# Two of w_ada's column blocks (j = 8 and 9) summed by VectorE instead of by column-grouped matmuls on TensorE

## The chip, the cores and the metric

One core of a Trainium2 chip runs the whole kernel. The metric is device microseconds of one execution, the median over several runs. Every time below is in microseconds (us) unless it is marked ns. The engines are called PE (TensorE matmul), PEld (its weight loads), DVE (VectorE), ACT (ScalarE), POOL (GpSimd) and SP (SyncE, which here only issues DMAs).

## The reference, cut to what matters

The kernel is one decoder layer on 512 tokens of 1024 channels. Its conditioning is one row of 6144 numbers:

```python
mod = jnp.einsum('bd,de->be', jax.nn.silu(c), w_ada[l]) + b_ada[l]
sh_m, sc_m, gt_m, sh_f, sc_f, gt_f = jnp.split(mod[:, None, :], 6, axis=-1)
...
u = layer_norm(x) * (1.0 + sc_f) + sh_f
```

With c of shape (1, 1024), this is a product of a vector with a 1024 x 6144 matrix in float32. Around it stand an input projection, two causal mixers (softmax attention with a forget bias, and an RG-LRU), an output projection and a mixture of 16 experts.

## The kernel before, in words

**Blocks of w_ada.** The 6144 columns are cut into twelve blocks j = 0 to 11 of 512 columns. Block j holds half of one of the six vectors: 0 and 1 sh_m, 2 and 3 sc_m, 4 and 5 gt_m, 6 and 7 sh_f, 8 and 9 sc_f, 10 and 11 gt_f. Each block comes in four quarters kh = 0 to 3 of 256 rows, 512 KB a DMA, which lie in SBUF as tile `wa` of 128 x 2 x 512 float32 (`ada_quarter`, L250 to L253). silu(c) lies in the tile `cb`, 128 x 8 x 32, each value repeated over 32 columns.

**Two ways to sum a block.** The string `ADA_BY` (L277) has one letter for each quarter of blocks 4 to 11, four to a block. `ada_acc(j, kh, w)` (L282 to L313) reads it. With "E" the quarters are gathered in pairs, and after kh = 1 and after kh = 3 PE runs four matmuls (L290; the trace has two instructions for each, so groups of eight), each with a stationary operand of 128 x 32 that writes one of four groups of 32 partitions of a PSUM tile; after kh = 3 ACT copies the PSUM tile to a tile `part` (L293). With "D" POOL zeroes `part` at the first quarter (L299), and each quarter costs two DVE instructions, `part = w[:, k, :] * cb[:, k] + part`, 128 x 512 (L305). Both leave a tile of 128 partitions that a later matmul sums over the partitions and turns into columns: `ada_T` (L315 to L323), whose column of weights for the sum is `s4` (one of each 32 partitions) for "E" and `ones1` for "D".

**When blocks are loaded and summed.** Blocks 0 to 3 are summed on PE at the start. From the first projection of the v columns on, each call of `proj()` takes up two quarters (`ada_next`, L482 to L491; `proj`, L493 to L510): blocks 6 and 7 go with the four v projections, block 8 with the projections of q and k of the first head pair (called q0 and k0 here), two quarters each. In `proj()` the quarters of a "D" block are summed by `ada_acc` ahead of that projection's matmuls in program order, and those of an "E" block behind them. Blocks 9, 10 and 11 stand in the hand-written list `TAIL` (L39 to L44): `AL` loads a quarter, `AC` sums one. Its beginning is

```python
AL, AL, pj(1, 0), AC, AC, AL, AL, pj(1, 1), AC, AC, T[0], S[1], N[1], AU[6], pj(2, 0), LW["L"], AL, GW("L", 0, V), GW("L", 1, V), FW["L"][0], pj(2, 1), AL, T[1], PV[0], S[2], AU[7], N[2], AC, AC,
```

Here `pj(i, 0)` and `pj(i, 1)` are the projections of q and k of head pair i; `S[n]` the logits of attention unit n (PE L851, L853, L856), their maximum (DVE L858) and exponential (ACT L861); `N[n]` the normalising (DVE L868, L871); `T[n]` the transposes of the probabilities (PE L883) and their split into a high and a low part (ACT L97, DVE L98); `PV[n]` the products with v; `LW`, `GW` and `FW` load, scale and split rows of w_out (DVE L743, ACT L748, DVE L749); `AU[j]` uses a finished block.

**What a projection waits for.** A projection's weight tile `wi` is loaded three projections ahead (`win_load`, L353 to L359): SP issues the DMA (L355), ACT makes the high part (L357), DVE the low part `wlo` (L358), and PE multiplies high and low parts in three products (L101 to L103). At its end ACT and DVE bring the result from PSUM into a pair of tiles (`qk_evac`: L665 and L666 for q, L668 and L669 for k).

**What sets the order.** The raw tiles `wa`, `wi` and `wo` share five buffers, so each load on SP waits until an earlier raw tile's last reader is done. SP and PE run in program order throughout. ACT, DVE and POOL are ordered by the framework's planner up to the point where `TAIL` begins (block 8 falls there), and in the order of the list from there on (block 9 falls there).

Of the kernel before, what the change touches and what calls it, by code (L numbers as in the profile page):

```python
# [47 lines left out]
def block_kernel(ctx, tc, x, c, w_ada, b_ada, w_in, b_f, conv_w, conv_b, w_rg, b_rg, w_ig, b_ig,  # L48
# [44 lines left out]
    def ps(shape=(128, 512), dt=F32):  # L93
        return pp.tile(list(shape), dt, tag="ps", name=nm("ps"))
# [155 lines left out]
    def ada_quarter(j, kh, src=None, eng=None):  # L250
        w = src[kh] if isinstance(src, list) else raw([128, 2, 512], "wa", src)
        (eng or SP).dma_start(w, w_ada[0, kh * 256:(kh + 1) * 256, j * 512:(j + 1) * 512].rearrange("(k p) n -> p k n", p=128))
        return w  # L253
# [20 lines left out]
    shfT, scfT = sfT[:, 0:8], sfT[:, 8:16]  # L274


    ADA_BY = "EEEEEEEEDDDDDDDDEEEEEEEEEEEEEEEE"  # L277
    parts = {}

    part_q, part_p = {}, {}  # L280
# [1 line left out]
    def ada_acc(j, kh, w):  # L282
        if ADA_BY[(j - 4) * 4] == "E":
            part_q.setdefault(j, []).append(w)
            if kh % 2 == 0:
                return
            if kh == 1:
                part_p[j] = ps()
            for k in range(4):
                T.matmul(part_p[j][32 * k:32 * k + 32, :], cb[:, 2 * kh - 2 + k, :], part_q[j][kh - 1 + k // 2][:, k % 2, :], start=kh == 1, stop=kh == 3)  # L290
            if kh == 3:
                parts[j] = t2k([128, 512], F32, "part")
                A.copy(parts[j], part_p[j])  # L293
                if j in (4, 5, 10, 11):
                    A.dma_start(parts[j][1:2, :], b_ada[0:1, j * 512:(j + 1) * 512])
            return
        if j not in parts:
            parts[j] = t2k([128, 512], F32, "part")
            G.memset(parts[j], 0.0)  # L299
            if j in (4, 5, 10, 11):  # L300
                A.dma_start(parts[j][0:1, :], b_ada[0:1, j * 512:(j + 1) * 512])
        how, ck = ADA_BY[(j - 4) * 4 + kh], cb[:, 2 * kh:2 * kh + 2, 0:1]
        if how == "D":
            for k in range(2):
                V.scalar_tensor_tensor(parts[j], w[:, k, :], ck[:, k, :], parts[j], op0=OP.mult, op1=OP.add)  # L305
            return
        if how == "A":
            for k in range(2):
                A.mul(w[:, k, :], w[:, k, :], ck[:, k, :])
        else:  # L310
            G.tensor_mul(w, w, ck.to_broadcast([128, 2, 512]))
        for k in range(2):
            G.tensor_add(parts[j], parts[j], w[:, k, :])  # L313

    def ada_T(j, part, sel_=None):  # L315
        p = ps()
        for b in range(4):
            T.matmul(p[:, b:b + 1], part[:, b * 128:(b + 1) * 128], s4 if sel_ is None else sel_, start=True, stop=True)  # L318
        o, b0, dst, shift = (j % 2) * 4, *{0: (8, shT, True), 1: (16, sc1T, False), 3: (64, shfT, True), 4: (72, scfT, False)}[j // 2]
        if shift:  # L320
            V.tensor_add(dst[:, o:o + 4], p[:, 0:4], vt[:, b0 + o:b0 + o + 4])
        else:
            V.scalar_tensor_tensor(dst[:, o:o + 4], p[:, 0:4], 1.0, vt[:, b0 + o:b0 + o + 4], op0=OP.add, op1=OP.add)  # L323
# [158 lines left out]
    def ada_next(n):  # L482
        late = []
        for j, kh in ada_rest[:n]:
            a = j, kh, ada_quarter(j, kh)
            if ADA_BY[(j - 4) * 4] == "E":
                late.append(a)
# [22 lines left out]
    def ada_row2(j, part):  # L510
        p = ps()
        T.matmul(p, (s5 if ADA_BY[(j - 4) * 4] == "E" else ones1).to_broadcast([128, 128]), part, start=True, stop=True)
        o = slice((j % 2) * 512, (j % 2) * 512 + 512)
        if j < 6:
            V.tensor_scalar(gtm[:, o], p, 1.0, None, op0=OP.add)
        else:
            A.activation(gtf[:, o], p, AF.Identity, bias=1.0)
# [548 lines left out]
    def ada_use(j):  # L1066
        return lambda: ada_T(j, parts[j], None if ADA_BY[(j - 4) * 4] == "E" else ones1) if j < 10 else ada_row2(j, parts[j])

# [796 lines left out]
```

## Time and profile before

| what | value |
|---|---|
| median of 3 runs | 655.67 us (652.84 to 656.31) |
| the profiled execution's own time | 654.58 us |
| its span from first to last instruction | 652.8 us |
| PE busy | 600.1 us, 92% of the span |
| DVE busy | 453.3 us, 69% |
| ACT busy | 322.3 us, 49% |
| DMA | 165.65 MB, mean 254 GB/s |

How to read it: an engine's busy time is the union of its instructions' spans. The chain of waits is followed back from the last instruction, at each step to what released it. In a timeline, a line is: start, duration, engine, source line, operation, tiles, count, and in brackets the idle time of the engine before it and what ended that idle time. "granted clock" is the share of TensorE's full clock in a stretch.

### The profile page before, as it was taken

The page shows a single profiled execution, that of the slowest core. Times are in us where ns is not written, and L with a number is a line of the kernel's source. Part 1 is how long each engine was busy: PE and PEld are TensorE (multiplying, and loading weights), DVE is VectorE, ACT ScalarE, POOL GpSimd, SP SyncE. Part 2 cuts the span into 40 slices and gives each one's busy share as a digit, 9 for nine tenths or more (in the row PEclk, how much of TensorE's full clock was granted, in tenths as well). Part 3 has the DMA queues.
Part 4 walks back from the last instruction along what each step waited for, and adds up shares of the span by engine and source line. Part 5 has one row for each costly group of instructions (what it writes and reads, how often), then busy time and mean ns, then how long its engine had stood idle before and what let it go on. Part 6 is the DMA issues. An engine that isn't in the chain of part 4 may idle for free.

```text
span 652.8 us, 10217 instructions
## 1 busy us (share of the span) xinstructions
PE 600.1 (92%) x3537; PEld 440.2 (67%) x3537; DVE 453.3 (69%) x740; ACT 322.3 (49%) x512; POOL 180.0 (28%) x186
## 2 busy tenths in 40 slices
PE   4798999999999999989899999999999899999990
PEld 0455877777886888879677776676667577766550
DVE  6757869845744677787798576938686785895264
ACT  0344797344436364644577454445545464753150
POOL 8800002100000000142155353435354343743000
PEclk9899999999999999997899999999999899999996
DMA  9996136996347305375799979799989999999523
GB/s 311 340 266 201 36 117 196 283 276 199 115 166 285 113 4 191 110 278 197 234 332 380 389 233 349 271 328 350 359 285 346 367 377 363 370 385 368 151 104 124
DMA packets 90862, 165.65 MB, mean 254 GB/s; under 512 B 9351, under 2 KB 29943, under 8 KB 90808
## 3 DMA queue, kind: packets, MB, share of 16 engines
q1 hardware_dynamic: 84080, 150.06, 66.2%
q0 software_dynamic: 5024, 10.70, 6.3%
q10 hardware_dynamic: 1704, 4.21, 1.8%
q8 instruction: 29, 0.48, 0.3%
q14 instruction: 25, 0.20, 0.1%
HBM read 156.58 MB, written 12.39 MB: 259 GB/s over the span
## 4 chain that ended last, share of the span: by engine, by line
PE 62%; DMA 18%; DVE 10%; ACT 5%; issue 3%; ACTq 0%; POOL 0%; SPq 0%; POOLq 0%; DVEq 0%
PE ps L101 12%; PE ps L102 12%; PE ps L103 12%; PE ps L1418 7%; DMA er<-in_w_e_up_dram 6%; DMA er<-in_w_e_down_dram 4%; DMA er<-in_w_e_gate_dram 4%; DVE wlo L812 3%; PE ps L1434 2%; DMA wa<-in_w_ada_dram 2%; PE ps L290 2%; DMA wi<-in_w_in_dram 1%; PE ps L318 1%; ACT pr L861 1%; PE ps L883 1%
## 5 line engine op out<-in xcount | busy, mean ns | idle before, releaser
L812 DVE TENSOR_TENSOR wlo<-er,whi 128x1024 fp32r<-128x1024 f32 x91 | 143.9, 1600 | 28.8 <-ACT whi L811 27.1
L811 ACT CAST whi<-er 128x1024 fp32r<-128x1024 f32 x120 | 125.3, 1049 | 73.7 <-PE ps L103 67.0
L812 POOL TENSOR_TENSOR wlo<-er,whi 128x1024 fp32r<-128x1024 f32 x29 | 74.8, 2579 | 76.8 <-ACT whi L811 76.6
L101 PE MATMUL ps<-uh,whi 128*128 128x512 f32 x160 | 64.4, 403 | 0.0
L102 PE MATMUL ps<-wlo,xth 128*128 128x512 f32 x144 | 58.1, 403 | 5.1 <-POOL wlo L812 4.1
L103 PE MATMUL ps<-uh,wlo 128*128 128x512 f32 x160 | 62.6, 392 | 0.0
L102 PE MATMUL ps<-ul,whi 128*128 128x512 f32 x160 | 62.5, 390 | 0.0
L101 PE MATMUL ps<-whi,xth 128*128 128x512 f32 x144 | 58.9, 409 | 0.0
L1418 PE MATMUL ps<-er,xT 128*64 128x256 f32 x512 | 58.8, 382 | 0.0
L103 PE MATMUL ps<-whi,xtl 128*128 128x512 f32 x144 | 57.6, 400 | 1.2 <-DVE xtl L98 1.2
L1418 PEld LDWEIGHTS ps<-er,xT 128*64 128x64 f32 x512 | 35.4, 137 | 19.4 <-issue 1.9
L326 POOL TENSOR_TENSOR rA<-rA,nhalf 128x1 f32<-128x1 f32 x4 | 2.2, 549 | 157.0 <-DVE rA L917 157.0
L101 PEld LDWEIGHTS ps<-uh,whi 128*128 128x128 f32 x160 | 30.1, 188 | 11.9 <-issue 3.9
L358 DVE TENSOR_TENSOR wlo<-wi,whi 128x1024 fp32r<-128x1024 f32 x20 | 25.5, 1275 | 16.9 <-ACT whi L357 16.9
L102 PEld LDWEIGHTS ps<-wlo,xth 128*128 128x128 f32 x144 | 27.4, 190 | 12.7 <-POOL wlo L812 5.8
L357 ACT CAST whi<-wi 128x1024 fp32r<-128x1024 f32 x20 | 21.0, 1048 | 29.0 <-DMA wi<-in_w_in_dram 20.6
L102 PE MATMUL ps<-wlo,hth 128*128 128x512 f32 x80 | 32.6, 407 | 2.6 <-DVE wlo L812 2.6
L103 PEld LDWEIGHTS ps<-uh,wlo 128*128 128x128 f32 x160 | 30.0, 188 | 6.9 <-DVE wlo L358 0.5
L102 PEld LDWEIGHTS ps<-ul,whi 128*128 128x128 f32 x160 | 30.1, 188 | 6.5 <-issue 0.5
L101 PE MATMUL ps<-whi,hth 128*128 128x512 f32 x80 | 33.0, 412 | 0.0
L103 PEld LDWEIGHTS ps<-whi,xtl 128*128 128x128 f32 x144 | 27.5, 191 | 7.9 <-DVE xtl L98 1.6
L103 PE MATMUL ps<-whi,htl 128*128 128x512 f32 x80 | 32.2, 403 | 0.0
(414 smaller groups left out, 1248.9 us busy)
## 6 DMA issues: line engine op xcount, KB each, us to landing
er<-in_w_e_gate_dram SPq DMA_DIRECT2D x64, 512.0 KB, 9.6
er<-in_w_e_up_dram SPq DMA_DIRECT2D x64, 512.0 KB, 11.3
er<-in_w_e_down_dram SPq DMA_DIRECT2D x64, 512.0 KB, 10.7
wa<-in_w_ada_dram SPq DMA_DIRECT2D x44, 512.0 KB, 6.2
wi<-in_w_in_dram SPq DMA_DIRECT2D x20, 512.0 KB, 7.3
wo<-in_w_out_dram SPq DMA_DIRECT2D x8, 512.0 KB, 5.1
wa<-in_w_ada_dram ACTq DMA_DIRECT2D x4, 512.0 KB, 12.1
x<-in_x_dram SPq DMA_DIRECT2D x4, 512.0 KB, 6.2
```

Source lines behind the costliest of these rows:

```text
L101: T.matmul(o, l[0], r[0], start=start, stop=False)
L102: T.matmul(o, l[0], r[1], start=False, stop=False)
L103: T.matmul(o, l[1], r[0], start=False, stop=stop)
L290: T.matmul(part_p[j][32 * k:32 * k + 32, :], cb[:, 2 * kh - 2 + k, :], part_q[j][kh - 1 + k // 2][:, k % 2, :], start=kh == 1, stop=kh == 3)
L318: T.matmul(p[:, b:b + 1], part[:, b * 128:(b + 1) * 128], s4 if sel_ is None else sel_, start=True, stop=True)
L357: A.copy(hl[0], r)
L358: V.tensor_sub(hl[1], r, hl[0].bitcast(F32))
L811: A.copy(hl[0], r)
L812: (eng or V).tensor_sub(hl[1], r, hl[0].bitcast(F32))
L861: A.activation(pr[j][:, n, :], lg_[j][:, n, :], AF.Exp, bias=nmx[:, j, n:n + 1], accum_out=ss[:, j, n:n + 1])
L1418: T.matmul(p[64 * h:64 * h + 64, :], xT[:, k, :], ws[w0 + k // 2][:, k % 2, h * 256:(h + 1) * 256], start=k == 0, stop=k == 7)
L1434: T.matmul(py[64 * h:64 * h + 64, :], hT[:, k % 2, (k // 2) * 64:(k // 2) * 64 + 64], ws[8 + k][:, h * 512:(h + 1) * 512], start=k == 0, s ...
```

## The change

Letters 16 to 23 of `ADA_BY` belong to blocks 8 and 9. They turn from "E" to "D"; nothing else is edited. Blocks 4, 5, 10 and 11 stay on PE, and 6 and 7 were on DVE already.

```diff
-    ADA_BY = "EEEEEEEEDDDDDDDDEEEEEEEEEEEEEEEE"
+    ADA_BY = "EEEEEEEEDDDDDDDDDDDDDDDDEEEEEEEE"
```

## Rows read from the trace of the kernel before

**Rows 1.** The page's first part: busy time, share of the span, instructions.

```profile
PE 600.1 (92%) x3537; PEld 440.2 (67%) x3537; DVE 453.3 (69%) x740; ACT 322.3 (49%) x512; POOL 180.0 (28%) x186
```

**Rows 2.** Busy time by stretch: PE, PEld, DVE, ACT, POOL, granted clock, DMA share, GB/s.

```profile
130.00:140.00 10.00, 10.00 (x54) 7.12 (x53) 5.05 (x7) 2.85 (x4) 0.00 (x0) 1.00 0.86 228
150.00:160.00 10.00, 10.00 (x62) 7.51 (x61) 4.40 (x6) 4.40 (x8) 0.00 (x0) 1.00 0.89 283
...
190.00:200.00 10.00, 9.59 (x72) 8.07 (x70) 5.97 (x12) 6.26 (x17) 0.00 (x0) 1.00 1.01 371
```

**Rows 3.** The chain of waits, 80 to 260 us: start, duration, what.

```profile
132.97 1.00 PE ps L290 x8
...
140.04 0.99 PE ps L290 x8
...
141.47 0.71 PE ps L853 x4
...
148.01 1.00 PE ps L290 x8
...
154.68 0.99 PE ps L290 x8
...
157.13 0.69 PE ps L853 x5
...
174.63 0.99 PE ps L290 x8
...
190.81 1.29 DVE pt L98 x2
```

**Rows 4.** DVE's timeline, 120 to 215 us.

```profile
131.41 1.22 DVE L358 TENSOR_TENSOR wlo<-wi,whi 128x1024 fp32r<-128x1024 f32 x1
135.32 1.22 DVE L358 TENSOR_TENSOR wlo<-wi,whi 128x1024 fp32r<-128x1024 f32 x1 [2.69 <-ACT whi L357]
...
140.70 0.69 DVE L669 TENSOR_TENSOR qk<-ps,qk 128x512 fp32r<-128x512 f32 x1 [2.96 <-ACT qk L668]
...
147.49 1.23 DVE L358 TENSOR_TENSOR wlo<-wi,whi 128x1024 fp32r<-128x1024 f32 x1 [1.80 <-ACT whi L357]
...
154.10 1.23 DVE L358 TENSOR_TENSOR wlo<-wi,whi 128x1024 fp32r<-128x1024 f32 x1 [4.67 <-ACT whi L357]
155.39 0.69 DVE L669 TENSOR_TENSOR qk<-ps,qk 128x512 fp32r<-128x512 f32 x1
156.92 1.29 DVE L98 TENSOR_TENSOR pt<-ps,pt 128x512 fp32r<-128x512 f32 x2 [0.84 <-ACT pt L97]
...
165.25 0.69 DVE L666 SCALAR_TENSOR_TENSOR qk<-ps,qk 128x512 fp32r<-128x512 f32 x1 [2.64 <-ACT qk L665]
...
168.35 1.28 DVE L749 SCALAR_TENSOR_TENSOR wlo<-wo,vt,whi 128x1024 fp32r<-128x1024 f32 x1
```

**Rows 5.** The SP queue's timeline, 128 to 215 us.

```profile
131.51 1.50 SPq L252 DMA_DIRECT2D wa<-in_w_ada_dram  x2
...
134.20 3.08 SPq L677 DMA_DIRECT2D brow<-in_b_grp_dram  x1
...
138.84 0.42 SPq L355 DMA_DIRECT2D wi<-in_w_in_dram  x1
...
148.74 0.99 SPq L355 DMA_DIRECT2D wi<-in_w_in_dram  x2
...
162.63 13.90 SPq L252 DMA_DIRECT2D wa<-in_w_ada_dram  x4
```

**Rows 6.** ACT's timeline, 120 to 215 us.

```profile
153.02 1.05 ACT L357 CAST whi<-wi 128x1024 fp32r<-128x1024 f32 x1 [4.31 <-DMA wi<-in_w_in_dram]
```

**Rows 7.** The tile `part`: instructions, count, duration in ns (min/median/max), first and last start.

```profile
L305 DVE SCALAR_TENSOR_TENSOR part<-wa,cb,part x16: 739/743/752, 108.7 to 130.7; 128x512 f32<-128x512 f32 x16
...
L293 ACT COPY part<-ps x6: 570/588/588, 95.2 to 210.2; 128x512 f32<-128x512 f32 x6
```

**Rows 8.** The tile `wa`, 100 to 220 us: time from a DMA's issue to landing.

```profile
DMA to landing us min/median/max: 3.8/5.0/9.7
```

## The prediction

> **What bounds the kernel now.** I read the page's busy shares first: PE is the busiest engine, 92% of the span against DVE's 69% [rows 1]. An average does not say what holds where the change is, so I took the busy times by stretch: from 130 to 160 us PE is busy all the time at full clock, DVE for 5.05 and 4.40 of 10 us in two stretches of it, POOL not at all [rows 2]. Then the chain of waits: all four L290 groups of blocks 8 and 9 stand on it, and so does the first product of q and k (L853) of attention units 0 and 1 behind them [rows 3]. From about 190 us on the chain leaves PE for ACT and DVE [rows 2, 3]. So in the changed region PE is the last to arrive, but the question is by how much. That is read from the timelines of DVE, SP and ACT [rows 4 to 6]: which of their results is ready just ahead of PE, and would hold it if PE came earlier.
>
> **The change, part by part.**
>
> *Removed on PE.* Four groups of eight matmuls: 1.00 + 0.99 + 1.00 + 0.99 = 3.98 us, all on the chain [rows 3]. ACT loses two copies of 0.588 [rows 7], off the path.
>
> *Added on DVE.* Sixteen products of 0.743 us [rows 7], 11.9 us, eight a block, 1.49 a quarter. POOL gets two memsets; it stands idle [rows 2], so I cost them at nothing; were POOL busy, the first product of each block would wait for them. PE's use of the finished block keeps its instructions. No DMA is added or dropped, but a buffer of `wa` is now freed by DVE instead of PE.
>
> *Block 8, up to unit 0's logits.* L853 of unit 0 starts at 141.47, right behind DVE's L669, which ends at 140.70 + 0.69 = 141.39 [rows 3, 4]. That is one of the two places where DVE is just ahead of PE. With the changed kernel, DVE is free at 131.41 + 1.22 = 132.63. Quarters 0 and 1 have landed or land then, 2.97 us of products to 135.60; the low part of the weights, 1.22 us, which before waited 2.69 us for ACT, then ends at 136.8 instead of 136.54 [rows 4]. Two more evacuations, 0.6 each from start to start, to 138.0. Quarters 2 and 3 are issued from 131.51 on, the second once the low part of 131.41 has ended at 132.63, so with the median landing of 5.0 they are there at 136.5 and 137.6 [rows 4, 5, 8]; 2.97 us more, to 141.0. If the planner puts L669 behind all of them, it ends at 141.7, 0.3 later than before, though PE was ready 1.99 earlier, at 139.48. If L669 goes ahead of the last two quarters, it ends near 140.4, 1.0 earlier: the projection is done at 140.04 - 1.00 = 139.04, and before it took 141.39 - 140.04 = 1.35 from there to the end of L669. I take the first, because `ada_acc` stands ahead of the evacuation in program order, and keep both for the range.
>
> *Block 9, up to unit 1's logits.* Before, L853 of unit 1 follows L853 of unit 0 by 157.13 - 141.47 = 15.66 us, of which 1.99 are the two L290 groups [rows 3]. From 141.8 PE would thus be there at 141.8 + 13.67 = 155.5. But unit 1 also needs L669 of this projection, which stands on DVE behind the low part of the next weights. That one ends at 154.10 + 1.23 = 155.33 because ACT waited 4.31 us for the weights' DMA, until 153.02; the DMA was issued at 148.74, at the very end of the low part of the weights before (147.49 + 1.23 = 148.72), whose raw buffer it takes; and those were issued at 138.84, behind an SP queue that spent 3.08 us on one small broadcast [rows 4 to 6]. Nothing in this chain of loads gets shorter when PE's groups go. DVE's four products of quarters 0 and 1, 2.97, fit into the 4.67 us in which it waited ahead of 154.10 [rows 4]. So L669 ends at 156.0 to 156.1 as before, and unit 1 starts there: 157.13 - 156.1 = 1.0 earlier. That is the gain. It is the same with either order at unit 0, and with unit 0 up to 0.6 later than I take it.
>
> *Block 9's second half.* Its four products stand on DVE behind L669 and in front of the splits of unit 0's probabilities: from 156.08 to 159.05, where before the first split began at 156.92. All that is queued behind them is 2.13 late: the splits, unit 1's maxima (for which ACT's exponentials wait), the last weights' low part, the scaling of w_out. PE needs none of these until its next two projections are through. DVE then idled 2.64 us ahead of the evacuation at 165.25 [rows 4]; in the changed kernel that evacuation is ready 1.0 earlier and DVE 2.13 later, so it starts at about 164.75, and the late time is used up. Were that idle time gone, 2.13 us would move on to the next thing that is late: the load of block 10's second quarter, which takes the buffer freed at 168.35 + 1.28 = 169.63 and is wanted by PE at 174.63 [rows 3, 4], 1.0 earlier in the changed kernel. With 0.5 earlier on DVE and 3.8 to 5.0 to land [rows 8] it is there between 172.9 and 174.1, against 173.6. I take 0, with up to 0.5 lost. On SP, two of the four w_out loads now wait until 157.6 and 159.05 for the buffers of quarters 2 and 3; behind them in that queue stands only block 10, whose first quarter waits for the last weights' low part in both kernels: issued at 162.63 before [rows 5], 2.13 later in the changed one, and landed 5.0 after that, at 169.8, early enough for 173.6.
>
> *Sum.* -3.98 on PE, of which 2.95 comes back as two waits for DVE (141.8 - 139.48 = 2.32 for unit 0, 156.1 - 155.47 = 0.63 for unit 1), 0 behind it: **-1.0 us**. From there to the end everything is released by something that moved with it, so I let 1.0 through. The profiled execution would go from 654.58 to 653.6; it lies 1.09 under the median of the runs shown, so the median goes from 655.67 to 654.7.
>
> **The rivals.**
>
> A, the whole gain: -3.98, 651.7 us. This needs L669 of unit 1 to come as early as PE, so the weights' load at 148.74 would have to start some 3 us sooner, for instance because the changed lifetimes give it a buffer that is free earlier. For it: PE is full and the groups lie on the chain [rows 2, 3]. Against it: that load is tied to the end of a low part that itself is tied to DMAs [rows 4 to 6]. The Trainium skill (Perfetto Trace Analysis, Identifying the Most-Contended Engine) says to improve the engine with the highest occupancy first; taken as a rule, that makes the whole of what leaves PE the gain. The trace agrees that PE is that engine [rows 1].
>
> B, the other side: DVE works in order, and the products get in front of a low part on which a load hangs. The place is the one of 131.41. If the planner puts quarters 0 and 1 ahead of it, it ends 2.97 late; with it the last load of block 8, the SP queue behind, the weights of 138.84, and by the same steps L669 of unit 1: 156.08 + 2.97 = 159.05, and unit 1 starts 1.9 later than before, 657.6 us. Were all four quarters ahead of the low part of 147.49 without any cover, 5.94 late, it would be +4.9, 660.6. It decides from the point where that low part ends later than 148.72 + 1.05, 1.05 being 157.13 - 156.08. For it: before 131 us DVE ran eight such products a block among the low parts and was full. Against it: DVE has 2.69 and 2.96 us idle where block 8 would go [rows 4], and quarters 0 and 1 are not there much sooner than 131. The Trainium skill (TensorE: Matmul & The Clock Gate, Engine queue depths) says that DVE's queue is strictly first in, first out; the low part of 154.10 with 4.67 us of idle time ahead [rows 4] agrees.
>
> C, that the letters belong to other blocks, has no chance: four letters a block from block 4 make letters 16 to 23 blocks 8 and 9.
>
> **How the numbers follow.** The forecast gets 0.64, A 0.13, B 0.19, and 0.04 is left for a reordering by the planner that I don't see. A measurement of this kernel can tell about 0.5%, 3.3 us, from no change. The forecast and the lower half of B lie within that; A (4.0) lies beyond, as do the upper half of B and part of the rest: faster 0.12, same 0.76, slower 0.12. The forecast's own range is 653.2 to 656.2 (unit 0's order, 0.5 for block 10, and the spread of the runs); with most of A and of B it is 651.6 to 658.6.
>
> **What would show it.** In the changed trace L290 has 16 instructions fewer per block and L305 32 instead of 16 at 0.74 us. Right: PE idle ahead of unit 0's or unit 1's L853 and released by DVE's L669; the weights issued at about 148.7; unit 1 about 1 us earlier; no wait for block 10. Wrong: no idle time on PE there and unit 1 near 153 to 154 (A), or the low part of 147.49 later than 149.8 with unit 1 behind 157.1 (B), or PE waiting at block 10's products.

## The result, and the profile after

The changed kernel takes 649.38 us (median of 8 runs, 646.45 to 651.58) beside 655.67 us of the kernel before on the same chip (8 runs, 650.86 to 656.86). The ratio on record is 0.9942 with an interval of [0.9919, 0.9965]: 655.67 x 0.0058 = 3.8 us faster, between 2.3 and 5.3. Each ratio of this document is made from the runs within 1.5% of their kernel's fastest (here all eight, in experiment 8 seven of twelve) and is not the quotient of the two medians, which here would be 0.9904, or 6.3 us. Timed a second time, against 35 runs of the kernel before, the ratio is 0.9964 [0.9939, 0.9990]. So it is faster by 0.4 to 0.6% by these ratios, where the forecast was -1.0 us or 0.15%: the sign is right, the size too small. The first timing is just beyond the half per cent named as the bound of no change, the second within it.

The page's first part of the changed kernel, to be held against [rows 1]:

```profile
PE 595.0 (92%) x3505; PEld 441.0 (68%) x3505; DVE 467.7 (72%) x756; ACT 321.2 (50%) x510; POOL 182.2 (28%) x188
```

PE has 32 instructions fewer, DVE 16 more, ACT two fewer, POOL two more. That is the change and nothing else. The profiled execution's own time is 647.57 us, its span 645.9 (652.8 before). These 6.9 us have two parts, and only the first can be put down to the change.

The chain of waits of the changed kernel, 80 to 260 us (start, duration, what), against [rows 3]:

```profile
140.96 0.61 DVE qk L669
141.62 0.73 PE ps L853 x4
...
154.94 0.89 PE ps L853 x5
...
172.55 1.00 PE ps L290 x8
...
188.73 1.29 DVE pt L98 x2
```

The four L290 groups of blocks 8 and 9 are gone (the one of 172.55 is block 10's). Unit 0's products start at 141.62 instead of 141.47: what block 8 had on PE has been given back in full. Unit 1's start at 154.94 instead of 157.13, 2.19 us earlier, and the same 2.1 is there at block 10's group (172.55 for 174.63) and at the split of 188.73 (190.81 before).

The chain of the kernel before, 262 to 620 us, at two products of the experts:

```profile
489.41 3.60 PE ps L1418 x32
...
542.23 3.60 PE ps L1418 x32
```

The same two in the changed kernel:

```profile
486.86 3.60 PE ps L1418 x32
...
535.51 3.60 PE ps L1418 x32
```

At the first the changed kernel is 2.55 us ahead, at the second 6.72. The 4.2 us between them come together with a fall of TensorE's clock. The stretches of the kernel before (behind the stretch, here and in [rows 2], stands its length; then PE, PEld, DVE, ACT, POOL, granted clock, DMA share, GB/s):

```profile
510.00:520.00 10.00, 9.71 (x43) 6.46 (x45) 6.20 (x8) 4.11 (x5) 2.61 (x2) 0.83 1.04 352
530.00:540.00 10.00, 8.91 (x40) 6.73 (x39) 8.97 (x9) 5.25 (x7) 2.70 (x1) 0.83 1.04 375
```

A granted clock of 0.83 over 10 us is 1.7 us of full clock less, 3.4 in the two. In both of them the changed kernel has a granted clock of 1.00, and so has the kernel before when it was profiled again (experiment 1). That second execution takes 541.13 - 491.40 = 49.73 us from the one product to the other, the first one 542.23 - 489.41 = 52.82, the changed kernel 535.51 - 486.86 = 48.65. So 3.1 of the 4.2 us came and went without any edit, and I don't count them to the change; what the other 1.1 us are is open. This pair of traces gives the change 2.1 to 2.5 us, which lies inside the second interval above (0.7 to 4.0 us) and at the edge of the first. It is one pair: a second execution of the changed kernel does not show this gain (experiment 1).

**Unit 0.** PE's timeline in the changed kernel:

```profile
139.29 0.49 PE L851 MATMUL ps<-ncum,sel 64*128 64x512 f32 x2
140.04 0.50 PE L853 MATMUL ps<-qk,qk 64*128 64x512 f32 x2 [0.25 <-ACT qk L668]
141.62 0.73 PE L853 MATMUL ps<-qk,qk 64*128 64x512 f32 x4 [1.07 <-DVE qk L669]
```

DVE's timeline of the same stretch:

```profile
131.36 1.22 DVE L358 TENSOR_TENSOR wlo<-wi,whi 128x1024 fp32r<-128x1024 f32 x1
132.50 3.10 DVE L305 SCALAR_TENSOR_TENSOR part<-wa,cb,part 128x512 f32<-128x512 f32 x4
135.52 1.22 DVE L358 TENSOR_TENSOR wlo<-wi,whi 128x1024 fp32r<-128x1024 f32 x1
...
137.86 3.10 DVE L305 SCALAR_TENSOR_TENSOR part<-wa,cb,part 128x512 f32<-128x512 f32 x4
140.88 0.68 DVE L669 TENSOR_TENSOR qk<-ps,qk 128x512 fp32r<-128x512 f32 x1
```

PE is through with the projection at 139.3 and stands until the last evacuation of k0 is done. That evacuation is at the end of a row of DVE instructions without one bracket: from 128.84 on DVE never idles, and L669 comes behind all eight products of block 8. Its input was ready at about 140.0, when ACT's half (L668, 139.40 + 0.58) was done, and it started at 140.88.

**Unit 1.** Here PE does not wait (154.78 in its timeline, no bracket). The forecast had DVE's L669 as the last to come, tied to a chain of loads. The links of that chain in the changed kernel, first on SP:

```profile
139.07 0.42 SPq L355 DMA_DIRECT2D wi<-in_w_in_dram  x1
139.58 1.77 SPq L252 DMA_DIRECT2D wa<-in_w_ada_dram  x2
147.62 3.84 SPq L355 DMA_DIRECT2D wi<-in_w_in_dram  x2
```

then ACT:

```profile
145.28 1.05 ACT L357 CAST whi<-wi 128x1024 fp32r<-128x1024 f32 x1 [0.55 <-DMA wi<-in_w_in_dram]
...
151.55 1.06 ACT L357 CAST whi<-wi 128x1024 fp32r<-128x1024 f32 x1 [2.65 <-DMA wi<-in_w_in_dram]
```

and DVE:

```profile
146.36 1.23 DVE L358 TENSOR_TENSOR wlo<-wi,whi 128x1024 fp32r<-128x1024 f32 x1 [0.52 <-ACT whi L357]
...
149.53 3.11 DVE L305 SCALAR_TENSOR_TENSOR part<-wa,cb,part 128x512 f32<-128x512 f32 x4
152.64 1.22 DVE L358 TENSOR_TENSOR wlo<-wi,whi 128x1024 fp32r<-128x1024 f32 x1
154.35 0.69 DVE L669 TENSOR_TENSOR qk<-ps,qk 128x512 fp32r<-128x512 f32 x1 [0.49 <-ACT qk L668]
154.96 3.10 DVE L305 SCALAR_TENSOR_TENSOR part<-wa,cb,part 128x512 f32<-128x512 f32 x4
157.99 1.28 DVE L98 TENSOR_TENSOR pt<-ps,pt 128x512 fp32r<-128x512 f32 x2
```

The two links that set the pace, before, on ACT and on SP:

```profile
146.40 1.05 ACT L357 CAST whi<-wi 128x1024 fp32r<-128x1024 f32 x1 [1.84 <-DMA wi<-in_w_in_dram]
```

```profile
141.06 0.88 SPq L252 DMA_DIRECT2D wa<-in_w_ada_dram  x2
```

The weights issued at 138.84 before [rows 5] and at 139.07 after reach ACT at 146.40 before and at 145.28 after: 7.56 us against 6.21. Everything behind follows: the next issue at 147.62 instead of 148.74, the low part at 152.64 instead of 154.10, and L669 waits for its projection (the bracket names ACT's half of the evacuation), no longer for the low part. What I see to differ near these weights is on SP: the two quarters of block 9 behind them. Before, PE's one group releases both buffers at once and the two loads are issued together, within 0.88 us. After, DVE releases one quarter 1.5 us ahead of the other, and the two issues are spread over 1.77 us. Experiment 8 says how far this goes as a cause. Part of the difference is chance: in its second execution the kernel before has 145.81 - 138.94 = 6.87 us there.

### The profile page after: what moved, and what is told of

Its sections match the earlier page's. It is cut to its first block, busy times and chain, and to the rows that moved or that the text cites. A ratio compares the mean times of both kernels' runs of the same rounds, so it can differ in the third digit from the quotient of the medians.

```text
span 645.9 us, 10172 instructions
## 1 busy us (share of the span) xinstructions
PE 595.0 (92%) x3505; PEld 441.0 (68%) x3505; DVE 467.7 (72%) x756; ACT 321.2 (50%) x510; POOL 182.2 (28%) x188
## 4 chain that ended last, share of the span: by engine, by line
PE 61%; DMA 13%; DVE 13%; issue 5%; ACT 5%; POOL 1%; ACTq 0%; SPq 0%; POOLq 0%; DVEq 0%
PE ps L101 12%; PE ps L102 12%; PE ps L103 12%; PE ps L1418 7%; DMA er<-in_w_e_up_dram 4%; DVE wlo L812 3%; DMA er<-in_w_e_down_dram 3%; DMA wa<-in_w_ada_dram 3%; PE ps L1434 2%; DMA wi<-in_w_in_dram 2%; DVE part L305 1%; PE ps L1034 1%; PE ps L883 1%; PE ps L290 1%; PE ps L318 1%
## 5 line engine op out<-in xcount | busy, mean ns | idle before, releaser
L812 DVE TENSOR_TENSOR wlo<-er,whi 128x1024 fp32r<-128x1024 f32 x91 | 149.0, 1656 | 25.0 <-ACT whi L811 25.0
```

The lines of the kernel that those rows point to most:

```text
L812: (eng or V).tensor_sub(hl[1], r, hl[0].bitcast(F32))
```

## The experiments

Four things were open. Does block 8 give back all it takes off PE, whatever happens in block 9? Does block 9 alone run into the load of the weights, as the forecast had it for both? What happens to TensorE's clock behind the new wait? And would another place for block 8's work, or a freer SP queue, give more? Each edit is shown against the kernel named with it. Ratios are to the kernel before on the same chip.

**1. The kernel before again, and the changed kernel again** (no edit).

> The kernel before, against itself: what a measurement of no change gives, and a second trace of it. Theory: ratio 1.000 with an interval that holds 1; the expert stage takes some us more or less than in the first trace, with its half-clock episodes in other places, and the weights issued near 138.8 land 1 us earlier or later than 146.3. Rival: the same half-clock episodes at 511 and 535 us, and the same landing.

> The changed kernel once more. Theory (the gain is made before 190 us and is about 2.2 us; the rest of the 6.9 us between the two profiled spans is two half-clock episodes in the expert stage of the one profiled execution before): attention unit 1 starts 2 us earlier than before, the offset stays at -2.0 to -2.4 from 190 us into the experts, and the measured ratio is 0.995 to 0.998 (-1.3 to -3.3 us). Rival (an earlier start also shortens the expert stage): the offset grows again between 500 and 545 us in this trace, and the ratio is 0.990 to 0.994.

Measured: 1.0010 [0.9979, 1.0041] and 0.9964 [0.9939, 0.9990]. The first is what no change looks like. Its trace has a granted clock of 1.00 in 510 to 520 and in 530 to 540 us. The changed kernel's trace (its longest execution of twelve, 655.05 beside a median of 649.93) shows something that its first one did not have. PE's timeline, and then the stretches behind it (columns as above):

```profile
142.66 0.73 PE L853 MATMUL ps<-qk,qk 64*128 64x512 f32 x4 [2.69 <-DVE qk L669]
...
156.12 1.03 PE L883 MATMUL ps<-ident,pr 128*128 128x128 f32 x8
...
157.42 1.05 PE L853 MATMUL ps<-qk,qk 64*128 64x512 f32 x6
```

```profile
142.00:146.00 4.00, 3.33 (x15) 2.66 (x16) 2.07 (x5) 1.67 (x5) 0.00 (x0) 0.74 1.08 349
146.00:150.00 4.00, 4.00 (x17) 3.23 (x16) 2.02 (x3) 0.76 (x1) 0.00 (x0) 0.83 0.57 193
```

In this execution a load of weights landed later, DVE's row started 0.74 later (the low part of 131.36 at 132.10), L669 came 1.05 later (141.93 for 140.88), and PE, which was 0.56 earlier than in the first trace, stood 2.69 us for it. Behind that wait TensorE was at its lower level, 1.2 GHz, for part of the next projection. From L853 to L883 this took 156.12 - 142.66 = 13.46 us, against 153.48 - 141.62 = 11.86 in the first trace: 1.6 us more. So the wait that the change puts there costs its own length, and in this execution 1.6 us of clock as well. With both, unit 1 starts at 157.42, behind both executions of the kernel before (156.97 and 156.53), and the split of 188.73 is at 191.37 (190.81 and 190.35 before). The 2 us that this run was expected to show are thus not in its trace, though they are in its ratio; how often an execution goes the one way or the other is not known.

**2. Block 8 alone.** Against the changed kernel:

```diff
-    ADA_BY = "EEEEEEEEDDDDDDDDDDDDDDDDEEEEEEEE"
+    ADA_BY = "EEEEEEEEDDDDDDDDDDDDEEEEEEEEEEEE"
```

> Block 8 alone on DVE, block 9 on PE as before. Theory (what PE saves on block 8 is given back at once, because unit 0's second half of k stands on DVE behind the block's last four products): unit 0's logits continue at 141.4 to 141.8 as before, the offset behind them is 0 to +0.3 us and the time is 0 to +0.3 us from before. Rival (each block that leaves PE counts): -2.0 us, ratio 0.997.

Measured: 1.0028 [0.9995, 1.0061]. PE's timeline and the stretch behind:

```profile
140.58 0.73 PE L853 MATMUL ps<-qk,qk 64*128 64x512 f32 x4 [1.36 <-DVE qk L669]
```

```profile
142.00:146.00 4.00, 4.00 (x12) 3.10 (x11) 2.87 (x6) 2.50 (x5) 0.00 (x0) 0.59 1.00 331
```

Block 8 brings nothing that can be told from noise: PE waits for L669 as forecast, and in this trace the lower clock follows, with a price of 1.6 us, 157.70 - 140.58 = 17.12 us to unit 1 against 156.97 - 141.47 = 15.50 before. The weights' load took 143.91 - 137.59 = 6.32 us, as in the changed kernel.

**3. Block 9 alone.** Against the changed kernel:

```diff
-    ADA_BY = "EEEEEEEEDDDDDDDDDDDDDDDDEEEEEEEE"
+    ADA_BY = "EEEEEEEEDDDDDDDDEEEEDDDDEEEEEEEE"
```

> Block 9 alone on DVE, block 8 on PE as before. Theory (its whole saving stays): -2.0 to -2.2 us from unit 1 on, as much as with both blocks, ratio 0.9965 to 0.997. The step as predicted (unit 1 is held by the second half of k, which hangs on the weights' DMA chain): -1.0 us, PE idle ahead of unit 1. Rival (each block counts the same): -2.0 us, half of what both give.

Measured: 0.9990 [0.9965, 1.0014]. Three lines, from the timelines of ACT, DVE and PE:

```profile
152.99 1.05 ACT L357 CAST whi<-wi 128x1024 fp32r<-128x1024 f32 x1 [4.04 <-DMA wi<-in_w_in_dram]
```

```profile
154.07 1.23 DVE L358 TENSOR_TENSOR wlo<-wi,whi 128x1024 fp32r<-128x1024 f32 x1 [1.27 <-ACT whi L357]
```

```profile
155.95 0.73 PE L853 MATMUL ps<-qk,qk 64*128 64x512 f32 x4 [0.71 <-DVE qk L669]
```

This is the forecast's picture of unit 1, to 0.15 us: the weights come at 153.0, the low part at 154.07, and PE waits for L669 until 155.95. With block 8 on PE the weights of 139.25 took 146.86 - 139.25 = 7.61 us, as before. Here too the lower clock follows the wait (0.60 in 158 to 162 us). So 0.28% lost by one block and 0.10% won by the other are not what both give together (0.36 and 0.58% won). Against the smaller of the two the gap is 0.5%, hardly more than the intervals leave open. The traces name two things that can stand behind it: the weights' load, which was slow in this trace as in the two of the kernel before, and the lower clock, which followed the wait in both of these executions but only in one of the two of the changed kernel.

**4. Work on PE ahead of the wait.** Six matmuls of 128x512 between k0's projection and unit 0's logits, in the changed kernel; their result is not used.

```diff
+    fill = ps()
+    for _ in range(6):
+        T.matmul(fill, uh[:, 0, 0:128], uh[:, 1, :], start=True, stop=True)
```

> The changed kernel with six more matmuls (128 x 128 by 512, their result unused) on PE between the projection of k of head pair 0 and unit 0's logits, where PE waits for DVE. Theory (PE's wait there is followed by a stretch at half clock in some executions, which costs some 1.7 us): granted clock 1.00 from 138 to 150 us, the wait shorter by 1.4 us, unit 0's L853 at the same time as in the changed kernel or at most 0.3 later, and the time 0 to 1.7 us below the changed kernel's. Rival (the half clock at 142 to 147 us is chance and has nothing to do with the wait): half clock there as often as with the changed kernel, time as the changed kernel's or 0.3 us above.

Measured: 0.9963 [0.9944, 0.9983]. PE's timeline and the stretch behind:

```profile
139.04 1.52 PE L1077 MATMUL ps<-uh 128*128 128x512 f32 x6
...
142.64 0.73 PE L853 MATMUL ps<-qk,qk 64*128 64x512 f32 x4 [1.42 <-DVE qk L669]
...
154.49 1.03 PE L883 MATMUL ps<-ident,pr 128*128 128x128 f32 x8
```

```profile
142.00:146.00 4.00, 3.36 (x19) 2.79 (x20) 2.05 (x5) 1.45 (x4) 0.00 (x0) 1.00 1.09 350
```

By chance this execution has DVE as late as the one of experiment 1 (unit 0 at 142.64 and 142.66). With the filler the clock stays at 1.00, and L883 comes at 154.49 instead of 156.12. This fits a clock that falls with the idle time and not with the late L669; but it is one execution each, and two without the filler kept their clock as well (waits of 1.07 us in the first trace and 1.11 in experiment 5). In the times the filler shows nothing (0.9963 beside 0.9964 and 0.9942 without), and intervals of 0.2% or more to either side would hide most of a 1.6 us that only some executions pay. That stays open.

**5. One quarter of block 8 on POOL**, in the changed kernel (a "G" is multiplied and added by POOL):

```diff
-    ADA_BY = "EEEEEEEEDDDDDDDDDDDDDDDDEEEEEEEE"
+    ADA_BY = "EEEEEEEEDDDDDDDDDDDGDDDDEEEEEEEE"
```

> The changed kernel with the last quarter of block 8 multiplied and added on POOL instead of DVE. Theory (PE waits at unit 0 for L669 because block 8's last products stand ahead of it on DVE): L669 starts 1.2 to 1.5 us earlier, unit 0's logits go on 0.9 to 1.5 us earlier, PE's wait there shrinks to about 0.7 us, and the time is 0.9 to 2.5 us below the changed kernel's. Rival (L669 is late for another reason, the ACT half or the weights): unit 0 within 0.3 us of the changed kernel.

Measured: 0.9973 [0.9949, 0.9996]. No gain is seen, and the trace has a reason of its own for it. POOL's timeline, DVE's, and the tile `part` (ns, min/median/max):

```profile
137.75 1.90 POOL L311 TENSOR_TENSOR wa<-wa,cb 128x1024 f32<-128x1024 f32 x1 [19.75 <-DVE qk L666]
```

```profile
137.84 3.14 DVE L305 SCALAR_TENSOR_TENSOR part<-wa,cb,part 128x512 f32<-128x512 f32 x2
140.89 0.68 DVE L669 TENSOR_TENSOR qk<-ps,qk 128x512 fp32r<-128x512 f32 x1
```

```profile
L305 DVE SCALAR_TENSOR_TENSOR part<-wa,cb,part x30: 737/746/2353, 109.2 to 157.3; 128x512 f32<-128x512 f32 x30
```

DVE had two products instead of four to do, and they took 3.14 us instead of 3.10, because the first took 2.35 instead of 0.75: it started 0.09 behind POOL's multiply of 1.90 us. L669 was at 140.89, as without the edit.

**6. A freer SP queue, block 9 alone.** The broadcast that held SP for 3.08 us [rows 5] and three small loads beside it are issued by POOL, or by SP later, ahead of the rows of w_out. Against the kernel before:

```diff
-    ADA_BY = "EEEEEEEEDDDDDDDDEEEEEEEEEEEEEEEE"
+    ADA_BY = "EEEEEEEEDDDDDDDDEEEEDDDDEEEEEEEE"
-    SP.dma_start(wr[:, :, 0:4], w_grp[0].rearrange("(k p) n -> p k n", p=128))
+    G.dma_start(wr[:, :, 0:4], w_grp[0].rearrange("(k p) n -> p k n", p=128))
...
```

> Block 9 alone on DVE, and the four small loads of the router's weights and biases issued by POOL instead of SP, so that SP does not spend 4 us on them ahead of block 9's quarters and the weights. Theory (unit 1 is held by L669, which hangs on the weights' DMA chain behind these loads, as the prediction's step has it): the weights are issued 2 to 4 us sooner, PE has no wait ahead of unit 1, no half clock near 158 us, and the time is 2.0 to 2.4 us below before, 1 to 2 us below block 9 alone. Rival (unit 1 waits for DVE's products): PE's wait of 0.7 us stays, time as block 9 alone.

The later variant, likewise against the kernel before with block 9 on DVE:

```diff
-    SP.dma_start(wr[:, :, 0:4], w_grp[0].rearrange("(k p) n -> p k n", p=128))
...
+    def small_loads():
+        SP.dma_start(wr[:, :, 0:4], w_grp[0].rearrange("(k p) n -> p k n", p=128))
...
+            if n == "woL":
+                small_loads()
```

> Block 9 alone on DVE, and the four small loads of the router's weights and biases issued by SP three projections later, ahead of w_out's rows, so that nothing early in the kernel changes. Theory (unit 1 is held by L669 behind the weights' DMA, and that behind SP's small loads): the weights are issued 2 to 4 us sooner, no wait of PE ahead of unit 1, unit 1 2.0 us earlier than before against unit 0, and 2.0 us below before, ratio 0.9965 to 0.9975. Rival (PE's wait of 0.7 us comes from DVE's products): the wait stays, ratio as block 9 alone (0.999).

Measured: 0.9992 [0.9974, 1.0010] and 0.9980 [0.9941, 1.0020]. In both traces PE has no wait at either unit and a granted clock of 1.00 all the way, and from unit 0 to unit 1 it takes 156.73 - 143.43 = 13.30 and 156.08 - 142.81 = 13.27 us, against 156.97 - 141.30 = 15.67 before. So block 9 can give all it has once the weights are there. But in both unit 0 itself comes 1.5 to 2.1 us later than before, which takes most of that back in these two executions. With POOL's issues part of this can be the edit's: the planner moved them to the start, from 19.35 us on, and a load of weights that SP issued at 29.42 before is issued at 31.61 (and at 31.59 in the kernel of experiment 7 with the same issues). With the late issues it is not: PE is 0.7 us late at 27.83 (27.12 before), far ahead of the place where the loads stood, and the next experiment's kernel, the same up to there, has unit 0 at 141.32.

**7. Block 11 as well.** The two kernels of experiment 6, and the changed kernel with the loads issued later, each with block 11 on DVE too:

```diff
-    ADA_BY = "EEEEEEEEDDDDDDDDEEEEDDDDEEEEEEEE"
+    ADA_BY = "EEEEEEEEDDDDDDDDEEEEDDDDEEEEDDDD"
```

> As the kernel with block 9 on DVE and the small loads moved, with block 11 on DVE too, whose four quarters are summed near 207 and 224 us, where DVE idles 5 us. Theory (a block's 2.0 us stay gained where nothing that PE waits for stands behind its products): 1.5 to 2.0 us below that kernel, 3.5 to 4.4 us below before. Rival (DVE's products delay the evacuations and splits of units 5 to 8): within 0.5 us of that kernel or above it.

> The same with block 11 on DVE too. Theory: another 1.5 to 2.0 us off between 205 and 230 us, 3.5 to 4.0 us below before, ratio 0.994 to 0.995. Rival (the products delay the later units' splits): at most 0.5 us below the kernel with block 9 and late small loads.

> Blocks 8, 9 and 11 on DVE with the late small loads. Theory (block 8 gives back at unit 0 what it saves): within 1 us of the kernel with blocks 9 and 11, PE waits 1 to 2 us at unit 0. Rival (block 8's 2.0 us count as well): 1.5 to 2.0 us below that kernel.

Measured: 0.9987 [0.9957, 1.0017], 0.9984 [0.9947, 1.0020] and 0.9971 [0.9934, 1.0008]. None can be told from the changed kernel, nor from the kernel before. PE's timeline of the second (its lines are numbered one higher):

```profile
141.32 0.87 PE L854 MATMUL ps<-qk,qk 64*128 64x512 f32 x6
...
154.61 1.06 PE L854 MATMUL ps<-qk,qk 64*128 64x512 f32 x6
```

Here block 9 gives its gain in full: unit 0 is where it was before (141.30), unit 1 is 2.36 us earlier (156.97 before), and the split is at 188.59 (190.81). Block 11 adds next to nothing: from that split to the products of 226.22 this execution takes 37.63 us, that of experiment 6's late variant 227.99 - 190.09 = 37.90. Block 11's products have come onto this execution's chain of waits, behind a load of the bias row into `part` that takes 3.28 us there. In the times (0.9984) even block 9's 2.2 us do not stand out from the interval. In the third, unit 0 waits 2.39 us for L669 and the lower clock follows once more (granted clock 0.65 in 146 to 150 us).

**8. Half of block 8's products left out**, in the changed kernel:

```diff
-            for k in range(2):
+            for k in range(0 if j == 8 and kh > 1 else 2):
```

> The changed kernel with the four products of block 8's last two quarters left out (their part of the sum is missing, their loads stay). Theory (PE waits at unit 0 because these products stand ahead of L669 on DVE): L669 starts right behind its ACT half, 1.0 to 1.4 us earlier against the end of k's projection, PE's wait ahead of L853's second part shrinks from 1.1-2.7 us to 0.3 us or less, and the time is 1.0 to 2.5 us below the changed kernel's. Rival (the wait has another cause): the wait stays.

Measured: 0.9959 [0.9913, 1.0005]. Its profiled execution took 655.87 us, above the median of 653.72, so only the order of events up to unit 1 is read. PE's timeline, then SP's and ACT's:

```profile
139.46 0.74 PE L853 MATMUL ps<-qk,qk 64*128 64x512 f32 x4 [0.23 <-DVE qk L669]
...
155.04 0.74 PE L853 MATMUL ps<-qk,qk 64*128 64x512 f32 x4 [0.87 <-DVE qk L669]
```

```profile
137.89 0.46 SPq L355 DMA_DIRECT2D wi<-in_w_in_dram  x1
138.40 1.25 SPq L252 DMA_DIRECT2D wa<-in_w_ada_dram  x2
```

```profile
145.69 1.05 ACT L357 CAST whi<-wi 128x1024 fp32r<-128x1024 f32 x1 [3.11 <-DMA wi<-in_w_in_dram]
```

Unit 0 hardly waits now and comes 2.2 us ahead of the changed kernel (1.3 of it this execution has already at L851, 137.99 for 139.29), and unit 1 is not a bit earlier: 155.04 beside 154.94, with PE waiting 0.90 and 0.87 us there. Here the letters are those of the changed kernel, but the last two quarters have no reader to release them one by one; the two loads of block 9 are issued within 1.25 us, and the weights take 145.69 - 137.89 = 7.80 us. So it is not the letter that makes the weights quick. Over nine traces: with the two loads issued together (before twice, block 9 alone, this one) the weights reach ACT 6.87 to 7.80 us after their issue; with the two apart (the changed kernel twice, filled, a quarter on POOL, block 8 alone) 6.21 to 6.32. Spacing alone does not decide it, though. In the traces of experiments 6 and 7, where other loads stand ahead, ACT took these weights later than they landed; by the landing itself the late variant of experiment 6 has 6.0 us with the two loads issued together, and the second kernel of experiment 7 has 7.7 with the two 1.77 apart (both pairs more than 4 us behind the weights). So what makes the weights quick in the changed kernel is not shown by these runs; that they come quicker there, and that it is not the letter by itself, is.

## Why the prediction was right or wrong

**Removed and added: right.** 3.98 us went from PE and sixteen products of 0.746 came to DVE.

**Block 8, up to unit 0's logits: right.** The planner did put L669 behind all eight products. Unit 0 was forecast at 141.8 and came at 141.62; experiment 2 shows it alone, with a gain of nothing. The Trainium skill's rule that DVE's queue is strictly first in, first out (TensorE: Matmul & The Clock Gate, Engine queue depths) is what one sees there: an evacuation whose input was ready at 140.0 stood until 140.88 behind products that nobody waited for. What the step left out is the clock. In four of six traces with such a wait and nothing put in its place (experiment 8 left out; the changed kernel again, block 8 alone, block 9 alone, the third of experiment 7) TensorE was at the lower level soon after, at a price of about 1.6 us in the two cases measured; in the six traces without a wait at these places (the kernel before twice and the first two of experiments 6 and 7) it was at 1.00 in 138 to 162 us.

**Block 9, up to unit 1's logits: the step that failed.** It said that nothing in the chain of loads gets shorter when PE's groups go, so that L669 ends at 156.0 to 156.1 as before, and unit 1 gains 1.0. Measured in the first pair of traces, unit 1 gains 2.19. The chain did get shorter, by 146.40 - 145.28 = 1.12 at its first landing and 153.02 - 151.55 = 1.47 at its second, which put the low part's end at 153.86 instead of the 155.33 of the step; from then on PE's own projection was last. The text had noted that a buffer of `wa` is now freed by DVE instead of PE, and had followed this for w_out behind block 9, but not for the loads of block 9 that block 8's buffers let in, which go out right behind the weights. That these are what made the weights quicker is likely and not shown (experiment 8). The step itself was sound for a kernel with block 8 on PE: experiment 3 shows it line by line. So the mechanism of the gain (PE's groups on the chain, the rest hidden) was right, and this term was sized at 1.0 instead of 2.2. In the second execution of the changed kernel (experiment 1) the weights were as quick, 6.28 us, and unit 1 was late all the same, because unit 0 was and the lower clock followed.

**Block 9's second half: right, at nothing.** DVE's late time was used up ahead of the evacuation L666 (163.58 in the changed kernel, 165.25 before [rows 4]; its 2.64 us of idle time is gone), and block 10 came 2.08 earlier with no wait.

**From there to the end: right in kind.** In the profiled pair the gain was let through: 2.19 at unit 1, 2.08 at 188.73, 2.55 at 486.86. What the pair shows beyond that is, for 3.1 of 4.2 us, the granted clock of one execution of the kernel before, in the experts.

**The rivals.** A, the whole gain, came halfway true: it asked for the weights' load to start some 3 us sooner, and it started 1.1 sooner, with unit 1 at 154.94, not at 153 to 154. Block 8's part of A did not come. B did not happen: the low part of 131.41 stayed ahead of the products (131.36), and nothing hung on it. The measured median, 649.38, is below both ranges; by the ratio it would be 655.67 x 0.9942 = 651.9, below the forecast's own range (from 653.2) and just inside the wide one (from 651.6). The 2.4 to 3.8 us of the two timings are not accounted for by traces: one pair shows 2.1 to 2.5 of them, the second execution of the changed kernel none. So that the sign came out is the mechanism's doing as far as the first pair shows it, and the size is not settled.

## What to carry to other kernels

When work leaves the bounding engine, ask twice where it goes: whether it stands on its new engine in front of something that the old engine waits for (block 8 did, and gave all back), and whose release of a buffer changes with it, since that moves the loads that the buffer lets in (here a load beside them came 1.1 us sooner, for a reason that these runs only narrow down). Make the edit's halves alone: two parts need not add up, here +0.28% and -0.10% alone against -0.4 to -0.6% together. Take a second trace before a gain of 2 us in 650 is read from one: here the second one did not have it. And where another limit stands close behind, freeing the first brings nothing while the second holds, as in experiment 8, where unit 0 came 2.2 us earlier and unit 1 did not.

## What the runs showed of the hardware

- A load of 512 KB reached its reader 6.2 to 6.3 us after its issue in five traces, where the issues of the two loads behind it were spread over 1.77 to 3.15 us, and after 6.9 to 7.8 in four, where they were spread over 0.88 to 1.25 us. With other loads ahead of it this did not hold (6.0 us with the two together, 7.7 with them apart).
- A wait of 0.7 to 2.7 us on PE was followed by a granted clock of 0.59 to 0.83 over the next stretch of 4 us in four executions out of six. The changed kernel itself shows both: after 1.07 us no fall, after 2.69 us one. With six matmuls put ahead of a wait as late, the clock stayed at 1.00.
- A DVE product of two SBUF tiles that took 0.75 us took 2.35 us beside a POOL multiply of 1.90 us. The Trainium skill (SBUF — State Buffer, SBUF: two separate sides) tells of a pair of ports shared by DVE and GpSimd, held by one for a whole instruction while the other stands. This trace agrees: 2.35 is about what was left of POOL's instruction (139.65 - 137.84 = 1.81) and a part of the product's own time behind it.
